# Two-layer memory hybrid in split fp32: how norms are summed and broadcast, where the forget gates are computed, and which instructions open a stage

## The chip, the cores and the metric

The kernel runs on one core of one Trainium2 chip. The metric is the device time of one execution in microseconds, as the median of several runs; the profile is of one more execution.

## The reference

A sequence of 512 tokens, width 1024, in fp32, goes through two layers, each a mixing step and a feed-forward step, all with RMS norms before and after:

```
for layer in range(2):
    a, mem_n = rmsnorm(h, ln_mix_pre[layer]), rmsnorm(mem, ln_mem[layer])
    if layer == 0:      # layer A
        u, v, q_mem = split(a @ w_in_a)                     # 768, 768, 256
        main = gelu(u) * (tril(w_s) @ layernorm(gelu(v)) + b_s)   # 6 groups, chunks of 128
    else:               # layer B
        k, v, f = split(rmsnorm(h, ln_shared) @ w_shared_kv)      # 768, 768, 12
        log_f = log_sigmoid(f + b_forget)                   # 12 heads
        q, q_mem = split(a @ w_in_b)                        # 768, 256
        c = cumsum(log_f)
        main = softmax(q k / 8 + c_t - c_s, causal) @ v     # forgetting attention
    mixed = concat(main, memory_attention(q_mem, mem_n, w_mem_kv))  # 4 heads, 256 memories
    h = h + rmsnorm(mixed @ w_out, ln_mix_post)
    f = rmsnorm(h, ln_ffn_pre)
    f = (silu(f @ w_gate) * (f @ w_up)) @ w_down            # inner width 2816
    h = h + rmsnorm(f, ln_ffn_post)
```

## The kernel before

Every large product is made of three products of split numbers: each fp32 value is held as a high part and a remainder, and `mm3` (lines 193 to 195) adds high x high, low x high and high x low in PSUM. The weights arrive from memory as `raw` blocks (queue of SyncE, SP, four buffers), ScalarE (ACT) casts the high part (`whi`, line 241) and VectorE (DVE) subtracts it (`wlo`, line 242). TensorE is PE below, GpSimd POOL. The program is written in Tile: the order of the code gives priorities, and a scheduler sets the order of instructions on each engine. `tc.issue_after(x)` pins the instructions in its block behind instruction `x`; `tc.high_priority()` lets them go ahead of what is written earlier.

The stages, in order:

- **Layer A.** Tokens and query weights are loaded and split as they come; the query product is made; then blocks of `v` (value_block, pieces of 12 matmuls), taken from a queue named `fill` wherever other work would leave PE waiting. The norm `pre` sums squares over the width (`add`), `finish` turns them with matmuls against a matrix of averages into one number a token (`st`, line 284) and raises it to -1/2 on POOL (`rsqrt`, line 256), `spread` broadcasts it over the partitions by a matmul against the identity (`rb`, line 252) and copies it. A second norm does the same for the memory.
- **Boundaries** (function `boundary`, three of them). `tail(tb)` closes the output product of a token block: DVE adds (line 770), ACT squares with a sum (773), DVE makes the variance `v` (775), POOL the power, ACT scales (792). `turn` transposes the scaled rows on PE (`yt`, line 799), adds them to `h` (804) and prepares the next stage's inputs, with squares folded by `PairNorm` (lines 311 and 313). `group` runs the next projection's first blocks, with `finish` behind it.
- **Feed-forward.** Gate and up products use seven block products instead of eight (class `Seven`): `sums` (lines 944 to 949) makes sums of weight blocks on DVE, `run` the products, `end` the output sums (lines 982 to 985). The hidden width goes in groups; between two groups stands part of the down product `y`. `sevens` runs one pair of blocks, gate and up.
- **Layer B.** Queries, then the forget gates, keys and values, the four memory heads and the twelve heads of the forgetting attention. The gates are a product of their own: `w_f` split into 24 columns (`wfs`), 16 matmuls `f` (line 1185), four transposes `zt` (1190), sums and bias into `z` (1201); then log-sigmoid on ACT and DVE (1204 to 1216: absolute value, exponential, logarithm, corrections), six pieces of `fill`, and the cumulated sum `cs` by matmuls with a triangle (1223), whose parts `cc` go by DMA into the rows 66:68 and 64:66 of the heads' operands `qc` and `kc` (1254, 1255). The heads' softmax uses the exponential on ACT (`mp`, `p`, line 432), `mlg` are the memory heads' logits, `tr` the transposes of the probabilities, `mo` and `o` the products with values. ACT loads a table of functions where the function changes.

## Time and profile before

| | us |
|---|---|
| median of 3 runs | 1131.65 |
| lowest, highest run | 1131.46, 1133.57 |
| profiled execution, span from first to last instruction | 1130.7 |
| mean granted TensorE clock in it | 0.999 |

The profiled execution is given by its span alone; the runs are timed on the device around such a span. How to read the rows: a row of a timeline has the start and the duration in us, engine, line, operation, output and inputs, and in brackets how long the engine sat idle before it and what ended that. A row of groups ends in count, busy time in us, mean ns of one, and idle time ahead. A row of the chain has start, length and what ran. Matmuls overlap: a 128x256 one takes 0.28 us from issue to its modelled end, and the next one starts 0.12 us after it.

### The profile page before, as it was taken

Reading aid. Unit: us, or ns where it says so; the run is one execution under the profiler, and the core shown is the slowest. Engines: PE = TensorE matmul, PEld = TensorE weight load, DVE = VectorE, ACT = ScalarE, POOL = GpSimd, SP = SyncE. Lnnn points to the kernel's source line nnn. Section 1 sums busy time; section 2 is a strip of 40 time slices with the busy share of each in tenths; the row PEclk is TensorE's granted clock in tenths of the full one; section 3 lists DMA queues with packets and bytes.
Section 4 is the critical chain, followed back from the end, with each engine's and each line's share of the span. In section 5 each row is a group of like instructions: output and inputs, shape, how many; then the busy total and the mean of one; then the engine's idle time right before and its main releaser. Section 6 shows DMA issues by size and latency. Waiting matters only on the chain.

```text
span 1130.7 us, 19666 instructions
## 1 busy us (share of the span) xinstructions
PE 1116.5 (99%) x7470; PEld 1015.8 (90%) x7471; DVE 893.1 (79%) x1717; ACT 662.2 (59%) x1385; POOL 24.7 (2%) x42
## 2 busy tenths in 40 slices
PE   9999999999999999999999999999999999999997
PEld 6998889999899898998988898889999899898995
DVE  7878558897698587796858889958998688588775
ACT  8774468664365264476637667768765266254453
POOL 1000000000000000000000000000000000000000
PEclk9999999999999999999999999999999999999999
DMA  7513222334134223343323455521224234133222
GB/s 262 159 38 113 89 79 76 112 111 132 57 112 149 64 87 112 98 152 107 96 93 90 112 128 135 137 75 57 68 102 150 75 104 135 62 112 113 75 75 75
DMA packets 63559, 118.14 MB, mean 104 GB/s; under 512 B 5164, under 2 KB 39992, under 8 KB 63464
## 3 DMA queue, kind: packets, MB, share of 16 engines
q1 hardware_dynamic: 62584, 116.05, 33.1%
q8 instruction: 59, 0.97, 0.3%
q0 software_dynamic: 192, 0.52, 0.2%
q10 hardware_dynamic: 688, 0.31, 0.1%
q14 instruction: 36, 0.29, 0.1%
HBM read 104.71 MB, written 2.10 MB: 94 GB/s over the span
## 4 chain that ended last, share of the span: by engine, by line
PE 88%; DVE 4%; ACT 3%; issue 2%; DMA 2%; POOL 1%; SPq 0%; POOLq 0%; DVEq 0%
PE y L195 9%; PE y L194 9%; PE y L193 9%; PE a L195 5%; PE a L194 5%; PE a L193 5%; PE ps L193 4%; PE ps L195 4%; PE ps L194 4%; PE e L193 3%; PE e L195 3%; PE e L194 3%; PE x L195 3%; PE x L194 3%; PE x L193 3%
## 5 line engine op out<-in xcount | busy, mean ns | idle before, releaser
L241 ACT CAST whi<-raw 128x512 fp32r<-128x512 f32 x460 | 276.7, 620 | 271.4 <-PE y L195 111.3
L242 DVE TENSOR_TENSOR wlo<-raw,whi 128x512 fp32r<-128x512 f32 x460 | 305.6, 685 | 113.2 <-ACT whi L241 109.2
L193 PE MATMUL y<-whi,fhi 128*128 128x512 f32 (+1 forms) x356 | 138.5, 390 | 0.9 <-DVE s L983 0.6
L194 PE MATMUL y<-wlo,fhi 128*128 128x512 f32 (+1 forms) x356 | 138.0, 388 | 0.3 <-DVE wlo L242 0.3
L195 PE MATMUL y<-whi,flo 128*128 128x512 f32 (+1 forms) x356 | 138.1, 388 | 0.1
L193 PE MATMUL x<-xshi,whi 128*128 128x256 f32 x320 | 90.6, 283 | 0.0
L194 PE MATMUL x<-xslo,whi 128*128 128x256 f32 x320 | 90.6, 283 | 0.0
L195 PE MATMUL x<-xshi,wlo 128*128 128x256 f32 x320 | 90.6, 283 | 0.0
L194 PE MATMUL a<-xslo,whi 128*128 128x256 f32 x320 | 90.5, 283 | 0.0
L193 PE MATMUL a<-xshi,whi 128*128 128x256 f32 x320 | 90.5, 283 | 0.0
L195 PE MATMUL a<-xshi,wlo 128*128 128x256 f32 x320 | 90.4, 283 | 0.0
L193 PEld LDWEIGHTS y<-whi,fhi 128*128 128x128 f32 x356 | 66.9, 188 | 15.4 <-DVE s L983 1.3
L195 PEld LDWEIGHTS y<-whi,flo 128*128 128x128 f32 x356 | 66.9, 188 | 14.6 <-DVE flo L242 1.1
L194 PEld LDWEIGHTS y<-wlo,fhi 128*128 128x128 f32 x356 | 66.9, 188 | 14.3 <-DVE wlo L242 1.2
L193 PE MATMUL ps<-xshi,whi 128*128 128x256 f32 (+1 forms) x224 | 67.8, 305 | 0.0
L195 PE MATMUL ps<-xshi,wlo 128*128 128x256 f32 (+1 forms) x224 | 66.8, 300 | 0.0
L194 PE MATMUL ps<-xslo,whi 128*128 128x256 f32 (+1 forms) x224 | 66.2, 298 | 0.0
L193 PEld LDWEIGHTS a<-xshi,whi 128*128 128x128 f32 x320 | 61.4, 192 | 0.3
L194 PEld LDWEIGHTS a<-xslo,whi 128*128 128x128 f32 x320 | 61.4, 192 | 0.3
L193 PEld LDWEIGHTS x<-xshi,whi 128*128 128x128 f32 x320 | 61.4, 192 | 0.0
L194 PEld LDWEIGHTS x<-xslo,whi 128*128 128x128 f32 x320 | 61.4, 192 | 0.0
L195 PEld LDWEIGHTS x<-xshi,wlo 128*128 128x128 f32 x320 | 61.4, 192 | 0.0
(292 smaller groups left out, 3115.6 us busy)
## 6 DMA issues: line engine op xcount, KB each, us to landing
raw<-in_w_gate SPq DMA_DIRECT2D x44, 512.0 KB, 4.2
raw<-in_w_up SPq DMA_DIRECT2D x44, 512.0 KB, 3.5
raw<-in_w_down SPq DMA_DIRECT2D x44, 512.0 KB, 3.7
raw<-in_w_out SPq DMA_DIRECT2D x16, 512.0 KB, 4.7
raw<-in_w_b_q SPq DMA_DIRECT2D x8, 512.0 KB, 3.5
raw<-in_w_a_v SPq DMA_DIRECT2D x6, 512.0 KB, 6.4
raw<-in_w_a_u SPq DMA_DIRECT2D x6, 512.0 KB
raw<-in_w_v SPq DMA_DIRECT2D x6, 512.0 KB, 3.4
```

The source lines that it names most:

```text
L193: PE.matmul(o, w[0], x[0], start=start, stop=False, skip_group_check=more)
L194: PE.matmul(o, w[0], x[1], start=False, stop=False, skip_group_check=more)
L195: return PE.matmul(o, w[1], x[0], start=False, stop=stop, skip_group_check=more)
L241: A.copy(hi, src)
L242: (eng or V).tensor_sub(lo, src, hi)
```

## The change

1. `broadcast` uses the transposing mode of PE instead of a matmul against the identity: one pass instead of two for each 128x128 block in fp32, at 18 blocks.
2. `PairNorm` folds its two halves with one more DVE add (128x256), so that `st` takes one matmul a token block instead of two (two passes instead of four). `finish` of a boundary's first half moves into `group`, behind its seventh step, and `group` gets a lag of 3.
3. Layer A: the squares of `pre` are pinned behind the last token's parts; its statistics are finished and spread once for all 512 tokens instead of in two halves, one value piece apart; the memory norm's `finish` comes three value pieces ahead of its `spread`. Value blocks that end before the statistics are queued (`evacs`).
4. Boundaries: the first two weight blocks are taken behind tail 0's weight parts, and the last tail's sums and scaling get high priority (`urgent`).
5. Feed-forward: the weight sums of a group's first block are pinned behind the last output sum of the group before (`opens`, `ended`); this holds for three groups a layer.
6. Forget gates: the 12 columns of `w_f` are appended to value block 0, whose matmuls become 268 columns wide; `z` is taken from its PSUM rows. The products `f`, the transposes and their copies are gone. The log-sigmoid (`forget`) stands among the memory heads' pieces after the second, the cumulated sum (`cumulate`) after the third, and the six pieces ahead of the heads move among them.

```diff
@@ -238,19 +238,25 @@
                 nc.sync.dma_start(dst, src)
 
     def split(src, hi, lo, eng=None):
-        A.copy(hi, src)
-        (eng or V).tensor_sub(lo, src, hi)
+        last_parts[:] = A.copy(hi, src), (eng or V).tensor_sub(lo, src, hi)
 
     def scaled_parts(src, g, hi, lo):
 
-        A.activation(hi, src, AF.Copy, scale=g)
-        V.scalar_tensor_tensor(out=lo, in0=src, scalar=g, in1=hi, op0=ALU.mult, op1=ALU.subtract)
+        last_parts[:] = (A.activation(hi, src, AF.Copy, scale=g),
+                         V.scalar_tensor_tensor(out=lo, in0=src, scalar=g, in1=hi, op0=ALU.mult, op1=ALU.subtract))
+
+    @contextmanager
+    def behind(some):
+
+        with ExitStack() as s:
+            for ins in some:
+                s.enter_context(tc.issue_after(ins.ins))
+            yield
 
     def broadcast(r4, tbs, o, c0):
 
         for tb in tbs:
-            PE.matmul(o[:, tb * P - c0 : (tb + 1) * P - c0], r4[:, tb : tb + 1].to_broadcast([P, P]),
-                      ident, start=True, stop=True)
+            PE.transpose(o[:, tb * P - c0 : (tb + 1) * P - c0], r4[:, tb : tb + 1].to_broadcast([P, P]), ident)
 
     def rsqrt(dst, src, n):
         G.tensor_tensor(out=dst, in0=src, in1=mhalf[:, :n], op=ALU.pow)
@@ -309,12 +315,14 @@
             c0, c1 = cols
             self.sq[j, cols] = prob("sq", (P, 2, 256))
             A.activation(self.sq[j, cols], h[:, 2 * j : 2 * j + 2, c0:c1], AF.Square)
+            t = self.sq[0, cols]
             if j:
-                V.tensor_add(self.sq[0, cols], self.sq[0, cols], self.sq[j, cols])
+                V.tensor_add(t, t, self.sq[j, cols])
+            if j == KT // 2 - 1:
+                V.tensor_add(t[:, 0, :], t[:, 0, :], t[:, 1, :])
 
         def sums(self, tb, cols):
-            c = slice(tb * P - cols[0], (tb + 1) * P - cols[0])
-            return [self.sq[0, cols][:, x, c] for x in range(2)]
+            return [self.sq[0, cols][:, 0, tb * P - cols[0] : (tb + 1) * P - cols[0]]]
 
 
     h = cp.tile([P, KT, T], F32, name="h")
@@ -596,9 +606,15 @@
                 for k in range(4 * kh, 4 * kh + 4):
                     mm3(o[tk], (a[k][0][:, c], a[k][1][:, c]), w[k], k == 0, k == KT - 1)
                 if kh:
-                    if tk % 2 == 0:
-                        vg[j, tk // 2] = plain("vg", (P, 2, 256))
-                    A.activation(vg[j, tk // 2][:, tk % 2, :], o[tk], AF.Copy, scale=pre.r4[:, tk : tk + 1])
+                    evacs.append(lambda: evacuate(tk))
+                if pre.done:
+                    while evacs:
+                        evacs.pop(0)()
+
+            def evacuate(tk):
+                if tk % 2 == 0:
+                    vg[j, tk // 2] = plain("vg", (P, 2, 256))
+                A.activation(vg[j, tk // 2][:, tk % 2, :], o[tk], AF.Copy, scale=pre.r4[:, tk : tk + 1])
 
             return load, [lambda tk=tk, kh=kh: piece(tk, kh) for tk in range(TB) for kh in range(2)]
 
@@ -611,30 +627,29 @@
                     end = mm3(o, w[k], a[k], k == 0, k == KT - 1)
                     if k == 0:
                         idle(2, zero, end)
-            for f in take(fill, 1):
-                f()
-            for k in range(KT):
-                pre.add(h[:, k, :])
-            for cols in HALVES:
-                pre.finish(cols)
+            def pieces(n):
+                for f in take(fill, n):
+                    f()
+
+            pieces(1)
+            with behind(last_a):
+                for k in range(KT):
+                    pre.add(h[:, k, :])
+            pieces(2)
+            pre.finish(FULL)
+            pre.done = True
             memt = load_mem()
-            for f in take(fill, 1):
-                f()
-            for cols in HALVES:
-                pre.spread(cols, rbc)
+            pieces(1)
+            pre.spread(FULL, rbc)
             qf = [plain("q") for _ in range(2)]
             for f, o in zip(qf, outs):
                 V.scalar_tensor_tensor(out=f, in0=o, scalar=0.125, in1=rbc, op0=ALU.mult, op1=ALU.mult)
             norm = mem_sums(memt)
-            for f in take(fill, 3):
-                f()
+            pieces(1)
             xs = mem_inputs(0, memt)
             wk = mem_key_weights(0)
-            for f in take(fill, 2):
-                f()
             norm.finish((0, NMEM))
-            for f in take(fill, 1):
-                f()
+            pieces(3)
             norm.spread((0, NMEM), rmem)
             V.tensor_copy(r4m, norm.r4[:, :2])
             q = [(act("q"), act("q")) for _ in range(2)]
...
+        def urgent(tb):
+            return tc.high_priority() if tb == TB - 1 and not last else ExitStack()
...
@@ -867,15 +889,19 @@
             c0, c1 = HALVES[half]
             return [tuple(t[:, c0:c1] for t in xs[k]) for k in range(KT)]
 
-        for tb in range(3):
-            tail(tb)
+        tail(0)
+        phase_parts = tuple(last_parts)
+        tail(1)
+        with behind(phase_parts):
+            ws = [block(n) for n in range(2)]
+        tail(2)
         turn(0, range(2))
         tail(3, lambda: turn(0, (2,)))
         turn(0, (3,))
-        ws = [block(n) for n in range(4)]
-        outs = group(ws, inputs(0), h0, ["mm", "lg"] * 2, lag=4,
-                     after={3: lambda: turn(1, range(2)), 5: lambda: turn(1, range(2, 4))})
-        nnorm.finish(h0)
+        ws += [block(n) for n in range(2, 4)]
+        outs = group(ws, inputs(0), h0, ["mm", "lg"] * 2, lag=3,
+                     after={3: lambda: turn(1, range(2)), 5: lambda: turn(1, range(2, 4)),
+                            6: lambda: nnorm.finish(h0)})
         nnorm.spread(h0, dst)
         evac(outs, h0)
         outs = group(ws[:2], inputs(1), h0, ["mm", "lg"])
@@ -982,15 +1008,20 @@
             V.tensor_add(s2[:, left], self.q, s2[:, left])
             V.tensor_add(s2[:, right], self.p, s2[:, right])
             self.rows(1, s2)
-            V.tensor_add(s1, self.x, s1)
+            end = V.tensor_add(s1, self.x, s1)
             self.rows(0, s1)
-
-    def sevens(pair, plain_first):
+            ended[0] = end
+
+    ended = [None]
+
+    def sevens(pair, plain_first, opens=False):
 
         if not plain_first:
             for make in pair:
                 u = make()
-                u.sums()
+                with behind(ended if opens else ()):
+                    u.sums()
+                opens = False
                 for n in (1, 7, 2, 6, 4, 3, 5):
                     u.run(n)
                 u.end()
...
-                                      lambda row, t: up_rows(row, t, fs))), m == 2)
+                                      lambda row, t: up_rows(row, t, fs))), m == 2, m == k0)
...
@@ -1148,86 +1179,83 @@
         def value_block(j):
 
             w, o = [], []
+            width = 256 + (0 if j else HEADS)
 
             def load():
                 for kh in range(2):
-                    w.extend(prepared(i["w_v"][j, kh], (4, 256)))
+                    if j:
+                        w.extend(prepared(i["w_v"][j, kh], (4, 256)))
+                        continue
+                    raw = loaded(i["w_v"][j, kh]).rearrange("p (a b) -> p a b", b=256)
+                    for x in range(0, 4, 2):
+                        pair = [t.rearrange("p (a b) -> p a b", a=2) for t in pair_of_parts(2 * width)]
+                        k = 4 * kh + x
+                        split(raw[:, x : x + 2, :], *(t[:, :, :256] for t in pair))
+                        split(wf[:, k : k + 2, :], *(t[:, :, 256:] for t in pair))
+                        w.extend(tuple(t[:, y, :] for t in pair) for y in range(2))
...
+                    if j == 0:
+                        V.scalar_tensor_tensor(out=z[:, tk, :], in0=o[tk][:, 256:], scalar=r4b[:, tk : tk + 1], in1=bf,
+                                               op0=ALU.mult, op1=ALU.add)
...
-        for k in range(KT):
-            w = wfs[:, k, :, :].rearrange("p a b -> p (a b)")
-            for x in range(2):
-                PE.matmul(o[:n2, :], w, s_act[k][x], start=(k, x) == (0, 0), stop=(k, x) == (KT - 1, 1))
...
-        for f in take(fill, 6):
-            f()
...
@@ -1271,7 +1300,9 @@
 
         ys, outs = out_part(1, mixed)
         more = queue(outs)
-        between = {n: take(fill, c) for n, c in enumerate((3, 3, 4, 4, 4, 4, 4, 4, 3, 3, 3, 3))}
+        between = {n: take(fill, c) for n, c in enumerate((5, 5, 5, 5, 4, 4, 4, 4, 3, 3, 3, 3))}
+        between[1].insert(4, forget)
+        between[2].insert(3, cumulate)
         for n, c in zip(range(12, 17), (2, 3, 3, 4, 4)):
             between[n] = take(more, c)
         assert not fill and not more
```

What the scheduler makes of it is shown at three places. First DVE at the opening of a feed-forward group in layer A (the fourth group). `raw` are weight blocks, `s_17` the sum of two of them, `s_16` the output sums of the block before. Before:

```order
L242 TENSOR_TENSOR wlo_5307<-raw_5304,whi_5306 128x512
L944 TENSOR_TENSOR s_17_5355<-raw_5346,raw_5348 128x512
L946 TENSOR_TENSOR raw_5348<-raw_5348 128x512
L983 TENSOR_TENSOR s_16_5059<-a_5056,s_16_5059 128x256
L985 TENSOR_TENSOR s_16_5058<-x_5055,s_16_5058 128x512
L1038 SCALAR_TENSOR_TENSOR s_16_5059<-s_16_5059,s_15_4922 128x512
L1040 TENSOR_TENSOR s_16_5058<-s_16_5058,s_15_4921 128x512
```

and now:

```order
L241 TENSOR_TENSOR wlo_5303<-raw_5296,whi_5302 128x512
L1009 TENSOR_TENSOR s_16_5051<-a_5048,s_16_5051 128x256
L1011 TENSOR_TENSOR s_16_5050<-x_5047,s_16_5050 128x512
L1069 SCALAR_TENSOR_TENSOR s_16_5051<-s_16_5051,s_15_4914 128x512
L1071 TENSOR_TENSOR s_16_5050<-s_16_5050,s_15_4913 128x512
L970 TENSOR_TENSOR s_17_5347<-raw_5338,raw_5340 128x512
L241 TENSOR_TENSOR flo_4905<-s_16_5051,fhi_4904 128x512
```

The weight sum moved from ahead of the output sums to four instructions behind. Second, ACT at the boundary behind layer A's mixing, with the last tail: `sq` with `ss` is the last square, `y` the scaling by `r`, `hs` and `xshi` the next stage's inputs. Before:

```order
L859 ACTIVATE hs_1972<-h,gains 128x256 x2
L311 ACTIVATE sq_1979<-h 128x512
L241 CAST xshi_1975<-hs_1972 128x512
L773 ACTIVATE sq_1996,ss_1757<-y_1754 128x512
L859 ACTIVATE hs_2009<-h,gains 128x256 x2
L792 ACTIVATE y_1673<-y_1673,r_1759 128x512
L792 ACTIVATE y_1754<-y_1754,r_1759 128x512
```

and now:

```order
L881 ACTIVATE hs_1986<-h,gains 128x256 x2
L317 ACTIVATE sq_1993<-h 128x512
L793 ACTIVATE sq_2010,ss_1751<-y_1748 128x512
L241 CAST xshi_1989<-hs_1986 128x512
L241 CAST whi_2036<-raw_2034 128x512
L814 ACTIVATE y_1667<-y_1667,r_1753 128x512
L814 ACTIVATE y_1748<-y_1748,r_1753 128x512
```

The last square moved ahead of one cast, and a weight cast took the place of the pair `hs` ahead of the scaling. Third, ACT in layer B, from the gates to the memory heads: `az`, `e`, `l` are the gates' steps, `lfh` the high part of the log gate, `mp` the heads' probabilities. Before:

```order
L1204 ACTIVATE az_6945<-z_6937 128x48
L1205 ACT_TABLE_LOAD
L1205 ACTIVATE e_6946<-az_6945 128x48
L1208 ACT_TABLE_LOAD
L1208 ACTIVATE l_1_6948<-w_1_6947 128x48
L241 CAST lfh_6960<-lf_6958 128x48
L241 CAST vals_6872<-vf_7009 128x4x64
L241 CAST vals_6873<-vf_7009 128x4x64
L1227 CAST cc<-cs_7074 12x512
L1229 ACTIVATE cc<-cc 12x512
L432 ACT_TABLE_LOAD
L432 ACTIVATE mp_7128,sm_7097<-mlg_7129,nmx_7096 128x256
```

and now, between the second and the third memory head:

```order
L440 ACTIVATE mp_7135,sm_6912<-mlg_7158,nmx_6911 128x256
L1230 ACTIVATE az_7180<-z_6900 128x48
L241 CAST vals_6863<-vf_7102 128x4x64
L1231 ACTIVATE e_7181<-az_7180 128x48
L241 CAST whi_7353<-q_6112 128x512
L1234 ACT_TABLE_LOAD
L1234 ACTIVATE l_1_7183<-w_1_7182 128x48
L241 CAST pT_7216<-tr_7215 128x512
L440 ACT_TABLE_LOAD
L440 ACTIVATE mp_7224,sm_6914<-mlg_7225,nmx_6913 128x256
L241 CAST pT_7237<-tr_7236 128x512
L440 ACTIVATE mp_7224,sm_6914<-mlg_7245,nmx_6913 128x256
```

The gates' steps moved from ahead of the heads to between their exponentials, with the table of the logarithm loaded there and the other one loaded back.

More of the change, by code (lines that the diff above doesn't have):

```diff
@@ L790, in tail @@
                 return end
[L791 to L792 removed]
+            with urgent(tb):
+                for y in ys[tb]:
+                    A.activation(y, y, AF.Copy, scale=r[:, c])
         return tail, ys
@@ L1219, in layer_b @@
-        cs = ps("mm", s="cs")
-        for tb in range(TB):
-            n = T - tb * P
-            for part in (lfh, lfl):
-                PE.matmul(cs[:HEADS, tb * P :], part[:, tb, :], tri[:, :n],
-                          start=(tb == 0 and part is lfh), stop=(tb == TB - 1 and part is lfl))
-        cc = tp.tile([P, T], F32R, tag="acc", name="cc", bufs=2)
-        ch, cl, nh, nl = (cc[32 * n : 32 * n + HEADS, :] for n in range(4))
-        A.copy(ch, cs[:HEADS, :])
-        V.tensor_sub(cl, cs[:HEADS, :], ch)
@@ new lines, in cumulate @@
+        def cumulate():
+            cs = ps("mm", s="cs")
+            lfh, lfl = sums["parts"]
+            for tb in range(TB):
+                n = T - tb * P
+                for part in (lfh, lfl):
+                    PE.matmul(cs[:HEADS, tb * P :], part[:, tb, :], tri[:, :n],
+                              start=(tb == 0 and part is lfh), stop=(tb == TB - 1 and part is lfl))
+            cc = sums["cc"] = tp.tile([P, T], F32R, tag="acc", name="cc", bufs=2)
+            ch, cl, nh, nl = (cc[32 * n : 32 * n + HEADS, :] for n in range(4))
+            A.copy(ch, cs[:HEADS, :])
+            V.tensor_sub(cl, cs[:HEADS, :], ch)
+            A.activation(nh, ch, AF.Copy, scale=-1.0)
+            V.tensor_sub(nl, ch, cs[:HEADS, :])
```

103 lines of the change are left out of this document (45 added, 58 removed).

## The prediction

> **What bounds the kernel now.** First, from the page of before, the busy shares and the shares of the chain that ended last:
>
> ```profile
> PE 1116.5 (99%) x7470; PEld 1015.8 (90%) x7471; DVE 893.1 (79%) x1717; ACT 662.2 (59%) x1385; POOL 24.7 (2%) x42
> ```
> ```profile
> PE 88%; DVE 4%; ACT 3%; issue 2%; DMA 2%; POOL 1%; SPq 0%; POOLq 0%; DVEq 0%
> ```
>
> TensorE (PE) is busy 99% of the 1130.7 us span and makes 88% of the chain. The kernel is a queue of matmuls: its time falls by what leaves that queue and by what the queue no longer waits for. Second, the waits of PE, longest first (total us, times, longest):
>
> ```profile
> PE yt L799 <- ACT y L792: 1.4, 3, 0.6
> PE idle L88 <- DVE zeros L80: 1.3, 1, 1.3
> PE mlg L465 <- ACT mp L432: 1.0, 1, 1.0
> PE rb L252 <- POOL r L256: 0.9, 2, 0.7
> PE y L193 <- DVE s L983: 0.6, 1, 0.6
> ```
>
> All but the start (`idle`) stand at places that the change touches. Each is understated: a wait is counted from the modelled end of the matmul before it, while the queue lost time from the moment at which the next one would normally have started. Third, therefore, the timelines around these places, by starts.
>
> **The work that leaves PE.** The forget gates, in PE's timeline:
>
> ```profile
> 584.92 0.40 PE L1185 MATMUL f<-shi,wfs 128*24 128x512 f32 x1
> 585.15 0.40 PE L1185 MATMUL f<-slo,wfs 128*24 128x512 f32 x1
> ```
> ```profile
> 588.61 0.28 PE L193 MATMUL v<-whi,shi 128*128 128x256 f32 x1
> 588.73 0.28 PE L194 MATMUL v<-wlo,shi 128*128 128x256 f32 x1
> ```
> ```profile
> 589.65 0.42 PE L1190 MATMUL zt<-ident,zr 24*128 24x24 f32 x4
> 590.00 0.39 PE L195 MATMUL v<-whi,slo 128*128 128x256 f32 x1
> ```
>
> The 16 `f` matmuls hold the queue from 584.92 to 588.61, 3.7 us; the four `zt` transposes from 589.65 to 590.00, 0.35 us. Both go. Instead the 96 matmuls of value block 0 (4 token blocks x 8 k x 3 products) are 268 columns wide. The next start follows 0.23 us after 512 columns (584.92 to 585.15) and 0.12 us after 256 (588.61 to 588.73): 0.11/256 us = 0.43 ns a column, so 96 x 12 columns cost 0.5 us. No row has 268 columns. The ends are no cost at all and the price of 512 columns, 96 x 0.11 = 10.6 us; I take 0.5, because 268 lies next to 256, and keep 10.6 for a rival. Net of this part: 3.7 + 0.35 - 0.5 = 3.5 us.
>
> The norms, in the timeline and, for the counts, in the groups of PE:
>
> ```profile
> 190.84 0.95 PE L284 MATMUL st<-avg,sq 128*128 128x1 f32 x8
> 191.65 0.36 PE L193 MATMUL ps<-xshi,whi 128*128 128x256 f32 x1
> ```
> ```profile
> 197.48 0.60 PE L252 MATMUL rb<-ident,r 128*128 128x128 f32 x4
> 197.84 0.47 PE L193 MATMUL y<-whi,fhi 128*128 128x512 f32 x1
> ```
> ```profile
> 606.65 1.03 PE L448 MATMUL tr<-ident,mp 128*128 128x128 f32 x8
> 607.44 0.48 PE L193 MATMUL k<-shi,whi 128*128 128x512 f32 x1
> ```
> ```profile
> L252 PE MATMUL rb<-ident,r 128*128 128x128 f32 x36 | 5.9, 285 | 0.9 <-POOL r L256 0.9
> L284 PE MATMUL st<-avg,sq 128*128 128x1 f32 x48 | 5.7, 240 | 0.0
> ```
>
> Eight `st` passes hold PE for 0.81 us. There are 48, six sets (two halves at three boundaries), and four of each eight go: 6 x 0.4 = 2.4 us. The DVE add that folds the two halves is 128x256, and one of that shape takes 0.42 us (L983, quoted below), six times. The chain that ended last shows its cover, the last fold of squares of a half and the sums behind it:
>
> ```profile
> 170.95 0.60 DVE sq L313
> ```
> ```profile
> 183.67 0.79 PE st L284 x8
> ```
>
> Twelve microseconds of projection lie between; with that cover gone the adds would cost 6 x 0.42 = 2.5 us.
>
> A broadcast (`rb`) of one block is two passes now; four hold PE for 0.36 us, 0.09 each. As a transpose it is one. The transposes `tr` of the memory heads hold it for 0.79 us by eight, 0.10 each. So 36 x 0.09 = 3.2 us become 18 x 0.10 = 1.8, and 1.4 us go. A transposed broadcast operand stands in no row; the ends are 0 and 1.6 (18 passes gone at 0.09), and I take 1.4 from the nearest row, `tr`.
>
> PE work removed: 3.5 + 2.4 + 1.4 = **7.3 us**. It is work of the queue itself, so it counts whole unless the queue waits anew.
>
> **The waits.** (1) The last tail at a boundary, in the timeline:
>
> ```profile
> 171.11 0.63 ACT L773 ACTIVATE sq<-y 128x512 bf16<-128x512 f32 x1
> ```
> ```profile
> 172.07 0.21 DVE L775 SCALAR_TENSOR_TENSOR v<-ss,rms_eps 128x1 f32<-128x1 f32 x1
> ```
> ```profile
> 172.82 0.28 PE L194 MATMUL ps<-xslo,whi 128*128 128x256 f32 x1
> 173.72 0.88 PE L799 MATMUL yt<-ident,y 128*128 128x128 f32 x6 [0.61 <-ACT y L792]
> ```
>
> PE should have gone on at 172.94 and went on at 173.72: 0.8 us, 0.17 more than the view's 0.61; the three of the group are so 1.4 + 3 x 0.17 = 1.9 us. In the new order of ACT the last square stands one cast (0.5 us) earlier; between it and the scaling lie two casts, about as long as the way over DVE and POOL (171.11 to 172.94 less the square's own time). So up to 0.5 us of each goes, **1.3 us** together (the shortest can't give all), and 0.6 is left. (2) The memory head's table:
>
> ```profile
> 600.40 1.28 ACT L432 ACT_TABLE_LOAD   x1
> ```
> ```profile
> 601.69 0.47 ACT L432 ACTIVATE mp<-mlg,nmx 128x256 f32<-128x256 f32 x1
> ```
>
> ACT loads the exponential's table behind the copies of the cumulated gates, and PE waits 1.0 us for that softmax. Now the heads begin before any gate's logarithm, with the table loaded ahead of the first logits: **1.0 us** goes. (3) The wait of `rb` for POOL, 0.9 us: the memory norm's statistics now lie three value pieces ahead of its broadcast (36 matmuls x 0.12 = 4.3 us), so this goes. By starts it is a little more, so I count **1.1 us**. (4) A group's opening:
>
> ```profile
> 437.28 0.39 PE L195 MATMUL y<-whi,flo 128*128 128x512 f32 x1
> 438.30 0.50 PE L193 MATMUL y<-whi,fhi 128*128 128x512 f32 x1 [0.63 <-DVE s L983]
> ```
> ```profile
> 436.49 0.69 DVE L944 TENSOR_TENSOR s<-raw,raw 128x512 f32<-128x512 f32 x1 [1.07 <-DMA raw<-in_w_gate]
> 437.22 0.69 DVE L946 TENSOR_TENSOR raw<-raw 128x512 f32<-128x512 f32 x1
> 437.83 0.42 DVE L983 TENSOR_TENSOR s<-a,s 128x256 f32<-128x256 f32 x1
> ```
>
> DVE stands 1.07 us for a weight block of the next group, then sums it, and only then finishes the products that PE needs: PE starts 1.02 us after its last start instead of 0.23. With the sums behind, 0.8 us goes here, and a little behind it: **1.0 us**. (5) At layer B's entry the same by way of ACT:
>
> ```profile
> 513.54 0.39 PE L195 MATMUL y<-whi,flo 128*128 128x512 f32 x1
> 514.16 0.49 PE L193 MATMUL y<-whi,fhi 128*128 128x512 f32 x1 [0.23 <-ACT whi L241]
> 514.97 0.50 PE L194 MATMUL y<-wlo,fhi 128*128 128x512 f32 x1 [0.31 <-DVE wlo L242]
> ```
>
> PE loses 0.4 + 0.6 us, counted from its normal 0.23 us between starts. ACT's queue holds casts of layer B's query blocks ahead of the tail's weights that PE waits for; these now stand behind: **0.9 us**. Together 1.3 + 1.0 + 1.1 + 1.0 + 0.9 = 5.3 us.
>
> Against it new waits. Layer A's two halves of statistics become one with a POOL power of four columns, and one value piece (12 x 0.12 = 1.4 us) lies between it and the broadcast; a 128x4 power takes 1.3 us on POOL, so there can be half a microsecond more. The value evacuations wait for that. ACT and DVE run in another order around each moved piece. From 0 to 3 us (the size of all that PE waits for here now); I take **1.0 us**.
>
> **The sum.** 7.3 + 5.3 - 1.0 = 11.6 us, on the span 1130.7 - 11.6 = 1119.1. The median of the runs, 1131.65, lies 0.95 us above the span, so **1120.0 us**.
>
> **Rivals.** *A: the work goes, the waits move.* A scheduler that reorders a whole program may end each wait and make another; then 7.3 us go, less up to 2: 1124.3 to 1126.3. For it: the waits are short, and DVE at 79% has slack but not much. Against: each has one cause in the rows, and the cause is moved.
>
> *B, slower: the pinned sums come too late.* The weight sums of the opening block now stand behind the last product sum, four DVE instructions later (4 x 0.6 = 2.4 us). The raw buffer is given back as much later, and the following load with its 4 to 5 us of landing. Six openings (three a feed-forward layer) at 2.4 us are 14.4 us, more than all that is won: 1120.0 + 14.4 = 1134.4. It decides once PE needs the block's sums less than 2.4 us after they were ready before. Against it:
>
> ```profile
> 458.51 0.28 PE L193 MATMUL a<-xshi,whi 128*128 128x256 f32 x1
> ```
>
> After the wait at 437 PE has the `y` of the old group to do until 458.51, 20 us.
>
> *C: the gates' logarithm between the exponentials.* The chain of the gates now runs between the second memory head's exponentials and the third's, with a load for the logarithm and one back. Each is 1.28 us, and the next ACT instruction starts 0.01 us behind it (600.40 + 1.28 = 601.68, and 601.69), so ACT loses 2.6 us where the softmax passes through it; the order leaves only some short matmuls as cover there, about 1 us as I estimate from their 0.12 us, so up to 1.6 us of it reaches PE: 1121.6. The Trainium skill ("ScalarE: Activation LUTs", "What ACT_TABLE_LOAD costs") counts 1.38 us of drain with each load, 2.66 us a switch. By it the two would cost 5.3 us and, past the same cover, 4.3 us: 1124.3. The row shows the 1.28 us but no idle time behind it; a drain ahead of it no run here separates.
>
> *D: the change doesn't do what it says.* If 268 columns are charged like 512 (10.6 us instead of 0.5), the time is 1130.1; if transposed broadcasts save nothing, 1121.4.
>
> **Chances.** Forecast, 1117 to 1122: 0.56. A 0.25, C 0.09 (inside the range), D 0.05, B 0.05. The range reaches down to **1116**, with no new wait and some unnamed ones mended, and up to **1126**, A with most of its new waits; left out are B, half of D and the edges, some 0.15. A measurement of this kernel tells 0.2%, 2.3 us, from no change. Faster by more: forecast, A, C and half of D, 0.92; same 0.03 (268 columns); slower 0.05 (B).
>
> **What would show it.** PE's page line should lose some 8 us of busy time. `f` and `zt` should be gone, `rb` be 18 and `st<-avg,sq` 24, and the `v` of value block 0 start 0.125 us apart. Waits of PE for `mp`, `r` and `s` should be gone and those for the scaled `y` half as long. I am wrong if PE waits in the memory heads for `pT` or at `cs` for `lfh`, if DVE waits for weight blocks at the openings and PE behind it, or if 268 columns start 0.2 us apart.

## The result, and the profile after

The changed kernel takes 1121.4 us, the median of 4 runs (1120.93 to 1122.15), against 1131.56 for the kernel before: a ratio of 0.9909, 95% interval 0.9895 to 0.9924. The forecast was 1120.0 us, 1116 to 1126. The profiled execution spans 1119.7 us, 11.0 less than before. On its page the busy shares and the shares of the chain:

```profile
PE 1107.3 (99%) x7409; PEld 1002.7 (90%) x7409; DVE 892.0 (80%) x1721; ACT 660.3 (59%) x1388; POOL 28.5 (3%) x41
```
```profile
PE 86%; DVE 7%; ACT 3%; issue 2%; POOL 1%; DMA 1%; SPq 0%; POOLq 0%; DVEq 0%; ACTq 0%
```

PE lost 9.2 us of busy time and stays the bound. One number on this line went up that the prediction never looked at: POOL is busy 28.5 us, 24.7 before, with one instruction fewer. The waits of PE, the longest first:

```profile
PE rb L259 <- POOL r L262: 2.5, 4, 1.7
PE idle L88 <- DVE zeros L80: 1.3, 1, 1.3
PE yt L821 <- ACT y L814: 1.0, 2, 0.5
PE ps L193 <- ACT whi L241: 0.7, 1, 0.7
PE e L193 <- ACT s L1003: 0.4, 1, 0.4
```

The waits for the table (`mp`), for the output sums (`s`) and for layer B's weights are gone. Those for the scaled rows (`yt`) fell from 1.4 to 1.0, not to half as was expected, and the wait of the broadcasts for POOL rose from 0.9 to 2.5, where it should have vanished.

To see where along the program the 11 us lie, the same matmul is looked up in both timelines of PE, and the difference of the starts is taken:

| the place | start before | start after | difference |
|---|---|---|---|
| behind the memory norm's broadcast, layer A (`ps<-mparts,wlo`) | 37.19 | 38.31 | +1.1 |
| ahead of the last tail, first boundary (`ps<-xshi,wlo`) | 172.01 | 174.54 | +2.5 |
| behind the second broadcast, first boundary (`y<-whi,fhi`) | 197.84 | 199.14 | +1.3 |
| layer B's entry, late (`y<-whi,fhi`) | 515.54 | 514.77 | -0.8 |
| behind the second boundary (`ps<-xshi,whi`) | 568.48 | 566.27 | -2.2 |
| layer B's output product (`y<-wlo,mixedhi`) | 745.96 | 738.55 | -7.4 |
| behind the third boundary (`y<-whi,fhi`) | 795.10 | 787.05 | -8.0 |
| the last `idle` matmuls | 1121.87 | 1112.67 | -9.2 |
| the end of the span | 1130.7 | 1119.7 | -11.0 |

The part of the work with the forget gates gives 5.2 us, the three boundaries 1.2, 1.4 and 0.6, the group openings and layer B's entry 2.1, the second feed-forward layer 1.2. Layer A loses 2.5: 1.1 up to the memory norm's broadcast and 1.4 behind it. Of the 1.4, 1.0 has nothing to do with layer A's new order: in the run below that widens the tiles of the weight parts and changes nothing else, the same matmul ahead of the last tail stands at 173.09 instead of 172.01, and the one behind the memory norm's broadcast at 37.25 instead of 37.19. And 1.8 us lie behind the last `idle` matmuls, where the change does nothing.

### The profile page after: what moved, and what is told of

The parts are those of the page before. It is cut to its first block, busy times and chain, and to the rows that moved or that the text cites. A ratio compares the mean times of both kernels' runs of the same rounds, so it can differ in the third digit from the quotient of the medians.

```text
span 1119.7 us, 19536 instructions
## 1 busy us (share of the span) xinstructions
PE 1107.3 (99%) x7409; PEld 1002.7 (90%) x7409; DVE 892.0 (80%) x1721; ACT 660.3 (59%) x1388; POOL 28.5 (3%) x41
## 4 chain that ended last, share of the span: by engine, by line
PE 86%; DVE 7%; ACT 3%; issue 2%; POOL 1%; DMA 1%; SPq 0%; POOLq 0%; DVEq 0%; ACTq 0%
PE y L193 9%; PE y L195 9%; PE y L194 9%; PE a L194 5%; PE a L193 5%; PE a L195 5%; PE ps L195 3%; PE ps L194 3%; PE ps L193 3%; PE e L193 3%; PE e L194 3%; PE x L194 3%; PE x L193 3%; PE x L195 3%; PE e L195 3%; DVE wlo L241 2%
```

## The terms, each as it ran

**The work that left PE** went as forecast. The new columns, the sums of a norm (four passes) and a broadcast (two blocks), each with the matmul that follows:

```profile
583.36 0.28 PE L193 MATMUL v<-whi,shi 128*128 128x268 f32 x1
583.48 0.28 PE L194 MATMUL v<-wlo,shi 128*128 128x268 f32 x1
583.60 0.29 PE L195 MATMUL v<-whi,slo 128*128 128x268 f32 x1
```
```profile
192.85 0.50 PE L290 MATMUL st<-avg,sq 128*128 128x1 f32 x4
193.21 0.37 PE L193 MATMUL ps<-xshi,whi 128*128 128x256 f32 x1
```
```profile
199.01 0.38 PE L259 MATMUL rb<-ident,r 128*128 128x128 f32 x2
199.14 0.48 PE L193 MATMUL y<-whi,fhi 128*128 128x512 f32 x1
```

A 268-column matmul gives way after 0.12 us; over all 96 the mean is 0.1237, so the columns cost 96 x 0.0037 = 0.35 us (forecast 0.5). The `st` set takes 0.36 instead of 0.81 us, six times 0.45 = 2.7 (forecast 2.4). The broadcast of two blocks takes 0.13 us here, 0.36 before; nine such pairs give up to 2.1 (forecast 1.4). With the 4.0 us of `f` and `zt` some 8.5 us went; 7.3 were forecast.

**The table** was loaded where the order said, and cost PE nothing. ACT's timeline between the heads:

```profile
601.39 0.62 ACT L241 CAST whi<-q 128x512 fp32r<-128x512 f32 x1 [0.37 <-PE k L194]
602.03 1.28 ACT L1234 ACT_TABLE_LOAD   x1
603.32 0.24 ACT L1234 ACTIVATE l<-w 128x48 f32<-128x48 f32 x1
603.47 0.57 ACT L241 CAST pT<-tr 128x512 fp32r<-128x512 f32 x1
604.06 1.28 ACT L440 ACT_TABLE_LOAD   x1
605.35 0.47 ACT L440 ACTIVATE mp<-mlg,nmx 128x256 f32<-128x256 f32 x1
```

Each load takes 1.28 us, begins 0.02 us behind the cast ahead of it and ends 0.01 us ahead of the next instruction. So the drain that the Trainium skill ("ScalarE: Activation LUTs", "What ACT_TABLE_LOAD costs") adds to each load, 1.38 us, isn't there on either side. PE waits for none of this: no wait for `mp`'s exponential is left in its list, and the one for the normalised `mp` in the list's tail is 0.3 us in layer A.

**POOL's power** is the term that came out on the wrong side. At the memory norm, the sums on PE with the matmul that follows, the power on POOL, DVE from the sums on, and the broadcast on PE:

```profile
29.02 0.95 PE L290 MATMUL st<-avg,acc 128*128 128x1 f32 x8
29.83 0.37 PE L193 MATMUL v<-whi,ahi 128*128 128x256 f32 x1
```
```profile
34.49 2.89 POOL L262 TENSOR_TENSOR r<-var,mhalf 128x2 f32<-128x2 f32 x1 [7.56 <-DVE var L292]
```
```profile
29.88 2.06 DVE L246 SCALAR_TENSOR_TENSOR mparts<-mem,gains,mparts 128x256 fp32r<-128x256 f32 x5
31.86 2.49 DVE L241 TENSOR_TENSOR wlo<-raw,whi 128x512 fp32r<-128x512 f32 x4
34.27 0.15 DVE L292 TENSOR_SCALAR var<-st 128x2 f32<-128x2 f32 x1
34.34 2.48 DVE L241 TENSOR_TENSOR wlo<-raw,whi 128x512 fp32r<-128x512 f32 x4
```
```profile
37.44 0.43 PE L259 MATMUL rb<-ident,r 128*128 128x128 f32 x2 [1.73 <-POOL r L262]
```

Two things came together. PE was done with the sums (`st`) at 29.83, but DVE made the variance `var` from them only at 34.27, 4.4 us later and behind nine other instructions (3.0 us later in the kernel before); by then the three value pieces that were to cover the way had run, and PE had work to 35.56. And the power took 2.89 us; the same shape took 1.19 before, and 0.69 to 0.70 at its shortest in both traces. It ran beside four subtractions on DVE and was done 0.56 us after the last of them.

Going through all powers in the two traces, the length goes with the DVE instruction that is running when the power starts. If there is none, or one of which an operand comes from PSUM (`h<-yt,...`, `y<-y`), a 128x1 power takes 0.54 to 0.57 us. If it is a subtraction or sum whose two operands both lie in SBUF (`xslo`, `wlo`, `hs`, `sq`), it takes 0.87 to 0.93, and a 128x2 one 0.98 to 2.89. The Trainium skill ("SBUF — State Buffer", "Who interferes with whom") says just that: a DVE instruction with two SBUF inputs contends with a GpSimd instruction that reads SBUF, and the second to issue waits until the first is done. By that alone the power would have been held for one subtraction. So it was at 555.54, where three subtractions follow each other too (1.08 us); at 194.20 it was held for two instructions (1.42 us), and here for four. What decides this, no run shows.

The same happened at the first and the third boundary, where the prediction counted 0.5 us each for the square that moved up:

```profile
174.15 0.21 DVE L795 SCALAR_TENSOR_TENSOR v<-ss,rms_eps 128x1 f32<-128x1 f32 x1
174.28 0.68 DVE L241 TENSOR_TENSOR xslo<-hs,xshi 128x512 fp32r<-128x512 f32 x1
```
```profile
174.44 0.92 POOL L262 TENSOR_TENSOR r<-v,mhalf 128x1 f32<-128x1 f32 x1 [7.52 <-DVE v L795]
```

Before, DVE stood idle beside this power and it took 0.54; now a subtraction starts 0.16 us ahead of it, and of the time won 0.4 us went back. By starts PE lost 0.77 and 0.76 us at these two boundaries before and loses 0.67 and 0.68 now. At the second boundary no such subtraction runs when the power starts; it keeps its 0.54 us, and PE's 0.4 us there are gone.

**The opening of a group** runs as planned: DVE's sums of the output come first, the weight sum (L970) last.

```profile
438.49 0.41 DVE L1009 TENSOR_TENSOR s<-a,s 128x256 f32<-128x256 f32 x1
438.82 0.68 DVE L1011 TENSOR_TENSOR s<-x,s 128x512 f32<-128x512 f32 x1
439.42 0.68 DVE L1069 SCALAR_TENSOR_TENSOR s<-s,s 128x512 f32<-128x512 f32 x1
440.02 0.68 DVE L1071 TENSOR_TENSOR s<-s,s 128x512 f32<-128x512 f32 x1
440.62 0.68 DVE L970 TENSOR_TENSOR s<-raw,raw 128x512 f32<-128x512 f32 x1
```

## The experiments

My theory, formed from the trace: the work counted whole, as forecast; of the waits, those whose cause was an order of DVE or ACT went, and those that hang on POOL's power did not, since DVE's subtractions hold it up. The rivals: the waits simply moved somewhere else; or the pins and the priority themselves cost what is missing.

**Layer A as before.** `layer_a` of the kernel before, all else of the changed one.

```diff
-            with behind(last_a):
-                for k in range(KT):
-                    pre.add(h[:, k, :])
...
-            pre.finish(FULL)
...
+            for cols in HALVES:
+                pre.finish(cols)
...
             norm.finish((0, NMEM))
-            pieces(3)
+            for f in take(fill, 1):
+                f()
```

> The changed kernel with layer A's opening as before (two halves of statistics, memory norm finished late). By the prediction's own sum the mended wait for POOL comes back, 0.9 us, less 0.5 us of dearer statistics: 1121.8 us. By the theory formed from the trace (a power on POOL is held up while DVE runs instructions with two operands in SBUF, so that the memory norm's power took 2.89 us after and 1.19 us before) the new order costs 1 us or more, and this kernel takes 1119.7 to 1120.5 us; the memory norm's wait of PE falls from 1.7 to 0.7 us.

Measured: 1120.34 us (ratio 0.9911, 0.9896 to 0.9925; the changed kernel has 0.9909). The wait fell as the theory said:

```profile
35.01 1.19 POOL L262 TENSOR_TENSOR r<-var,mhalf 128x2 f32<-128x2 f32 x1 [10.24 <-DVE var L292]
```
```profile
PE rb L259 <- POOL r L262: 0.9, 4, 0.4
```

The power is at its old 1.19 us and PE's wait for powers at 0.9 in all, 0.4 of it at the memory norm. The time is on the theory's side of 1121.4, not on the prediction's (1121.8), but the intervals overlap: layer A's new order won nothing. That it lost a microsecond rests on one profile of each: at the same matmul in layer A (`rows<-whi,tri`, 100.22 in the changed kernel) this one stands 1.3 us earlier, 0.4 of which it had already while the first tokens were loaded.

**The forget gates as before.** Layer B of the kernel before, part tiles 512 wide.

```diff
+                PE.matmul(o[:n2, :], w, s_act[k][x], start=(k, x) == (0, 0), stop=(k, x) == (KT - 1, 1))
...
-        between[1].insert(4, forget)
-        between[2].insert(3, cumulate)
```

> The changed kernel with the forget gates as before: own matmuls and transposes ahead of the memory heads, value block 0 at 256 columns, all part tiles 512 wide. By the prediction 3.5 us of PE work and 1.0 us of waiting for the table come back: 1121.4 + 4.5 = 1125.9 us. If the logarithm between the heads' exponentials costs what the rival said, up to 1.6 us, only some 3 us come back: 1124.4 us.

Measured: 1125.47 us (0.9947, 0.9934 to 0.9960), 4.1 us above the changed kernel, against 4.5 forecast and 3 with the rival's stall. The wait that the move had removed is back, whole:

```profile
PE mlg L473 <- ACT mp L440: 1.0, 1, 1.0
```

So the rival of the logarithm between the exponentials falls. The 4.1 us aren't the gates alone, since this kernel also has its part tiles back at 512 columns: behind the second boundary it stands 1.2 us ahead of the changed kernel (565.10 against 566.27), at layer B's output product 3.4 us behind it (741.93 against 738.55). In this stretch 4.6 us came back, against 4.5 forecast.

**No pins on the weight sums.**

```diff
-                                      lambda row, t: up_rows(row, t, fs))), m == 2, m == k0)
+                                      lambda row, t: up_rows(row, t, fs))), m == 2)
```

> The changed kernel without the pins on the weight sums of a group's first block. By the prediction the wait at the fourth group comes back, 0.8 to 1.0 us: 1122.3 us, with PE waiting for DVE's output sums at one opening. If late sums cost (the rival with the pins), it is faster than 1121.4 us, by up to 2.4 us an opening.

Measured: 1122.51 us (0.9921, 0.9908 to 0.9934): 1.1 above, as forecast, but with overlapping intervals, and the profile shows less. DVE's order is the old one, yet the load landed earlier against PE's work than in the kernel before:

```profile
437.26 0.69 DVE L970 TENSOR_TENSOR s<-raw,raw 128x512 f32<-128x512 f32 x1 [0.54 <-DMA raw<-in_w_gate]
437.98 0.69 DVE L972 TENSOR_TENSOR raw<-raw 128x512 f32<-128x512 f32 x1
438.59 0.42 DVE L1009 TENSOR_TENSOR s<-a,s 128x256 f32<-128x256 f32 x1
```
```profile
438.60 0.39 PE L195 MATMUL y<-whi,flo 128*128 128x512 f32 x1
439.07 0.50 PE L193 MATMUL y<-whi,fhi 128*128 128x512 f32 x1
```

PE loses 0.47 - 0.23 = 0.24 us at this start, where the row of before had 0.8. Over the whole opening it loses more: ahead of it (`y<-whi,fhi`, 437.14 in the changed kernel) this kernel stands 0.4 us earlier than the changed one, behind it (`y<-whi,flo`, 450.20) 0.2 us later, 0.6 in all. So the pins help by 0.6 us at this opening in one profile of each, and by 1.1 us in the medians; that the rest of the 0.8 came from the earlier load is likely and not shown. The rival with the late sums falls: without the pins the kernel isn't faster.

**The norms as before.** Broadcasts as matmuls, two sums a block, no fold.

```diff
-            PE.transpose(o[:, tb * P - c0 : (tb + 1) * P - c0], r4[:, tb : tb + 1].to_broadcast([P, P]), ident)
+            PE.matmul(o[:, tb * P - c0 : (tb + 1) * P - c0], r4[:, tb : tb + 1].to_broadcast([P, P]),
+                      ident, start=True, stop=True)
...
```

> The changed kernel with the broadcasts as matmuls against the identity and the norms' sums over both halves of the folded squares. By the prediction 2.4 + 1.4 us of PE work come back: 1125.2 us. If the power on POOL sets when PE goes on at each norm, fewer passes beside it only lengthen the wait, and it is 1123 us or less. If transposed broadcasts save nothing, 1123.8 us.

Measured: 1127.27 us (0.9965, 0.9953 to 0.9977), 5.9 us above. Of the 5.7 us between the two spans some 4.2 lie ahead of the last matmuls, against 3.8 forecast and 4.8 by the rows of the changed kernel; the other 1.5 lie behind the last matmul. So the passes count whole, also where PE waits for the power just ahead of them.

**The tile width in the kernel before.** In every run that holds the 268-column block PE's pace was another: the starts of 512-column products stood 232 ns apart instead of 227 (medians), those of 256-column ones 118.3 instead of 120.0 (means without the waits). The change widens the tiles of weight parts from 512 to 536 columns for all that share the tag, so only that was done to the kernel before.

```diff
-        return (wp.tile([P, 512], F32R, tag="hi", name=name("whi"), bufs=8)[:, :n],
-                wp.tile([P, 512], F32R, tag="lo", name=name("wlo"), bufs=8)[:, :n])
+        return (wp.tile([P, 536], F32R, tag="hi", name=name("whi"), bufs=8)[:, :n],
+                wp.tile([P, 536], F32R, tag="lo", name=name("wlo"), bufs=8)[:, :n])
```

> The kernel before with its weight part tiles allotted 536 columns instead of 512 (2144 bytes apart instead of 2048) and nothing else changed. If the place of these tiles sets PE's pace, the starts of 512-column matmuls stand 232 ns apart (227 before) and of 256-column ones 118 ns (120 before), as in every run that holds the 268-column block; 1928 x 5 - 4828 x 1.7 ns leaves the time within 2 us of 1131.4. If something else of the forget gates' part sets the pace, it stays at 227 and 120.

Measured: 1132.78 us (1.0011, 1.0001 to 1.0022), and the pace went over: 232 and 118.3 ns. One stretch of `y` in the kernel before and here:

```profile
277.96 0.39 PE L195 MATMUL y<-whi,flo 128*128 128x512 f32 x1
278.19 0.39 PE L193 MATMUL y<-whi,fhi 128*128 128x512 f32 x1
278.42 0.39 PE L194 MATMUL y<-wlo,fhi 128*128 128x512 f32 x1
278.64 0.39 PE L195 MATMUL y<-whi,flo 128*128 128x512 f32 x1
```
```profile
278.04 0.40 PE L195 MATMUL y<-whi,flo 128*128 128x512 f32 x1
278.28 0.40 PE L193 MATMUL y<-whi,fhi 128*128 128x512 f32 x1
278.51 0.40 PE L194 MATMUL y<-wlo,fhi 128*128 128x512 f32 x1
278.75 0.40 PE L195 MATMUL y<-whi,flo 128*128 128x512 f32 x1
```

Three products take 0.68 us and 0.71. That the allotted width of these tiles sets the pace is shown, since nothing else was changed; whether by where they lie or by what moves behind them isn't. Over the program it nearly cancels: 1928 x 5 = +9.6 us against 4828 x 1.7 = -8.2, and the median rose by 1.4 us (interval 0.1 to 2.5). Stage by stage it doesn't, as layer A's 1.0 us shows.

**Tiles of 544 columns**, a multiple of 64 bytes apart, in the changed kernel; and the same with the parts of the seven products moved by 32 bytes.

```diff
+    def pair_of_parts(n=512, aside=False, off=0):
...
+        return (wp.tile([P, 544], F32R, tag="hi", name=name("whi"), bufs=8)[:, off : off + n],
...
+            pair = pair_of_parts(off=8)
```

> The changed kernel with its weight part tiles allotted 544 columns instead of 536, so that they lie 2176 bytes apart, a multiple of 64 bytes. If it is the 32-byte offset of every second tile that sets the pace, it comes back to 227 and 120 ns; if the larger tile as such, it stays at 232 and 118. The time is within 1.5 us of 1121.4 either way.

> The same at 544 columns, with the parts of the feed-forward layers' seven products moved 32 bytes into their tiles and all others at its start. If the offset sets the pace, the 256-column matmuls of these products stand 118 ns apart or less and the 512-column ones 227: 2880 x 2 to 3 ns and 1800 x 5 ns under the changed kernel's, together some 10 us less than 1121.4: 1111 to 1113 us. If only the place of the whole set counts, nothing is won.

Measured: 1122.62 us (0.9926, 0.9911 to 0.9941) and 1122.83 us (0.9923, 0.9909 to 0.9938). The pace lies between: about 230 and 119.0 ns in both. So it is neither the 32-byte offset of every second tile alone nor the larger tile as such, and the 10 us that the second was to win aren't there. Which property of the address sets the pace stays open.

**No high priority for the last tail.**

```diff
-            return tc.high_priority() if tb == TB - 1 and not last else ExitStack()
+            return ExitStack()
```

> The changed kernel without the high priority of the last tail's steps. By the prediction 0.5 us of waiting at each of three boundaries comes back: 1122.7 us. If the power on POOL is held up by DVE's subtraction that now runs beside it (0.92 us against 0.54), the priority had won next to nothing, and the time stays within 0.5 us of 1121.4.

Measured: 1124.39 us (0.9941, 0.9927 to 0.9956), slower than either theory said. At the boundary itself the theory of the held power was right: with no subtraction beside it the power takes its short time again,

```profile
174.44 0.54 POOL L262 TENSOR_TENSOR r<-v,mhalf 128x1 f32<-128x1 f32 x1 [7.86 <-DVE v L795]
```

and behind the first boundary's second broadcast this kernel is 0.7 us ahead of the changed one (198.46 against 199.14), 0.35 of which it brought from the first loads. So the priority cost 0.35 us at this boundary; by the same count it cost 0.4 at the third and won 0.4 at the second, the one where the power stays short. The kernel loses its time at one opening:

```profile
PE y L193 <- DVE s L1009: 2.6, 1, 2.6
```

There ACT stood 4.30 us for a block of down weights, where the changed kernel's ACT stood 1.32. Whether that is this order or a late load of this execution is the question of the last run but one.

**The memory norm first.** The statistics right behind the squares, and the key weights' subtractions pinned behind the power.

```diff
...
             norm = mem_sums(memt)
+            power = norm.finish((0, NMEM))
             pieces(1)
             xs = mem_inputs(0, memt)
-            wk = mem_key_weights(0)
-            norm.finish((0, NMEM))
+            with behind((power,)):
+                wk = mem_key_weights(0)
             pieces(3)
```

> The changed kernel with the memory norm's statistics taken right after its squares, and the key weights' subtractions on DVE pinned behind its power on POOL. If the power is held up by subtractions with both operands in SBUF (2.89 us in the changed kernel), it now runs beside DVE's products of q, which read PSUM, in about 0.7 us, and PE's wait of 1.7 us at the memory norm's broadcast goes: 1121.4 - 1.7 = 1119.7 us. If something else makes the power long, it stays above 2 us; if the wait only moves to the next step, the time stays at 1121.4.

Measured: 1120.04 us (0.9894, 0.9879 to 0.9908), the fastest of all. On POOL and beside it on DVE:

```profile
28.45 0.71 POOL L262 TENSOR_TENSOR r<-var,mhalf 128x2 f32<-128x2 f32 x1 [1.77 <-DVE var L292]
```
```profile
28.21 0.16 DVE L292 TENSOR_SCALAR var<-st 128x2 f32<-128x2 f32 x1
28.28 1.28 DVE L646 SCALAR_TENSOR_TENSOR q<-ps,rbc 128x512 f32<-128x512 f32 x2
```
```profile
40.81 0.39 PE L194 MATMUL memv<-wlo,mparts 128*128 128x256 f32 x1 [0.89 <-DVE wlo L241]
```

DVE is as busy beside this power as it was beside the long one, but with products that read PSUM: 0.71 us instead of 2.89. The wait of 1.7 us at the broadcast is gone, and 0.9 of it comes back as a wait for a subtraction that now runs later. That the shorter power took the wait away isn't shown by this run: `var` now comes right behind the sums too, and even a power of 2.89 us from 28.45 would have ended at 31.34, 2.4 us ahead of the broadcast at 33.76. At the same matmul in layer A (`rows<-whi,tri`) this kernel stands 1.2 us ahead of the changed one, 0.3 of it from the first loads. It beats both others by its median; against the changed one the intervals overlap.

The same edit with layer A's opening as before:

> The same edit in the kernel with layer A's opening as before (1120.34 us). There the memory norm's broadcast waits least, so at most 0.9 us is left to win by the theory of the held-up power: 1119.4 to 1120.3 us.

Measured: 1121.5 us (0.9906, 0.9889 to 0.9922). The power is short there too (0.69 us), but the profile has a wait of 1.5 us at an opening of the second feed-forward layer and one of 1.0 us for the first tokens, both far from the edit. Inconclusive on the 0.9 us.

**The memory norm first, and no high priority.**

> The kernel with the memory norm's statistics first (1120.04 us) and without the high priority of the last tail's steps. If that priority wins little at the boundaries themselves and the 2.6 us at the first feed-forward group's opening were the chance of one late load, this takes 1119.5 to 1120.5 us and shows no such wait. If the order without the priority makes the down weights late each time, it takes 1122.5 to 1123.1 us, with PE waiting some 2.5 us for DVE's output sums at that opening.

Measured: 1121.53 us (0.9907, 0.9891 to 0.9924; single runs 1120.85 to 1125.28). The profiled execution, the one of 1125.28 us, has the wait again:

```profile
PE y L193 <- DVE s L1010: 3.4, 2, 2.9
```

The other three runs, 1120.85 to 1122.05, are too short to hold it: the shortest run without it, of the kernel with the norm first, is 1119.38 us, and 2.9 more would be 1122.3. So without the priority the down weights can come too late at that opening, but not each time. What the priority is worth is left open: it costs some 0.35 us over the three boundaries in the profiles, and wins up to 3 us by way of a load behind them.

**More instructions for PE.** The stretch from the last matmul to the end had followed the packets of instructions on queue 8 in the profiles up to here: 59 packets and 5.4 to 5.9 us in the kernel before, in the one with the old norms and in the padded one; 58 and 3.9 to 4.0 in the others.

```diff
     idle(10, zero)
+    o = ps("tr", s="idle")
+    for _ in range(80):
+        PE.matmul(o[:, :1], zero[:, :P], zero[:, :1], start=True, stop=True)
```

> The changed kernel with 80 more matmuls of one column at its start, on zeros, which PE runs while it waits for the first loads or just behind; nothing reads them. In the nine profiles so far the stretch from the last matmul to the end of the program is 5.4 to 5.9 us where queue 8 carries 59 packets of instructions (the kernel before and the two that hold most PE instructions) and 3.9 to 4.0 us where it carries 58. If the count of PE instructions sets this, the packets become 59 and the end 5.4 us or more, with a time of 1123 to 1129 us by what the 80 cost themselves; if it was something in the norms' code, they stay at 58 and 3.9.

Measured: 1121.91 us (0.9911, 0.9892 to 0.9931), 59 packets, and an end of 3.95 us. The packets don't set it. The end is long in the three kernels with the old norms and short in all others; why, no run shows.

## Why the prediction was right, and where it wasn't

- **The PE work** (7.3 us forecast, some 8.5 measured) is the bulk of the gain, and its working held term by term. The two experiments that put it back returned 4.6 us in the gates' stretch, with their table, and 4.2 us ahead of the last matmul for the norms.
- **The table** (1.0) and **layer B's entry** (0.9) held: neither wait is left, and the first came back whole when it was undone.
- **The opening of a group** (1.0): the wait is gone; without the pin 0.6 us came back at this opening in the profile.
- **The wait of `rb` for POOL** (1.1 to be won) is the step that failed: at the memory norm it grew from 0.7 to 1.7 us. The prediction set three pieces of PE's work, 4.3 us, against the way from the statistics to the broadcast and followed neither engine on that way. DVE came to `var` 4.4 us behind the sums, so the cover had run out when the power began; and the power, which the sum gave no length at all, was held to 2.89 us. By the times of the trace it took both: a power of 0.70 us from 34.49 would have ended at 35.19, ahead of the 35.56 to which PE had work, and one of 2.89 us right behind the sums at about 33. The other 0.6 of the 1.6 us by which the list grew is 0.3 at layer A's first norm, which the prediction allowed for among the new waits, and 0.3 at two boundaries.
- **The last tail** (1.3 to be won) was too large: 0.6 by starts, 0.4 in the list of waits. At the first and third boundary the power went from 0.54 to 0.92 us, and PE won only 0.1 us at each; at the second it stayed at 0.54, and the wait went.
- **New waits** (1.0 us taken): single ones of 0.2 to 0.7 us in the list of PE (`ps`, `e`, `tr` and `mo`), 1.6 us together, with an old one of 0.4 gone: about the size taken.
- **The pace** of PE is a term that the prediction doesn't have: the 536-column tiles slow the 512-column products and speed up the 256-column ones. In the kernel before, that cost 1.4 us by the median, and by the profile 1.0 us in layer A alone.
- The **waits** together were to give 4.3 us. The work took some 8.5 of the 9.2 us up to the last `idle` matmuls, so all else gave under 1. That the total still fits (11.6 forecast, 11.0 in the profile) is in part luck: it is owed to more work gone than counted and to 1.8 us behind those matmuls that the prediction knew nothing of. The case of rival A, that the waits move, is what half happened; the larger part of what moved, 1.6 us of the list, stands at POOL's powers.

## What to carry to other kernels

Before counting a wait as mended, follow every step of the way that is to be covered on its own engine, in that engine's order, and look at what runs beside it: here 4.3 us of PE's work were spent before DVE came to a step of 0.15 us, and the power behind it took 2.9 us beside DVE's subtractions instead of 0.7. Where a small POOL step lies on the path, put DVE work that reads PSUM beside it, as in the fastest kernel here, and keep subtractions of two SBUF operands behind it. And add up a profile by the starts of the same instruction at a few places of both traces, and of the traces of the experiments: the sum was right here while two of its terms were not, and only so did the part of the tile width show.

## What the runs showed of the hardware that was not expected

- A POOL power of 128x2 took 0.69 to 2.89 us by what DVE ran beside it. It was held for one, two or four DVE instructions in a row, with the same kind of instruction beside it; why, no run shows.
- The allotted width of the weight part tiles (2048, 2144 or 2176 bytes) sets PE's pace for all products that use them: 227, 232 and 230 ns for 512 columns, 120.0, 118.3 and 119.0 ns for 256. At 2048 bytes nine of ten 256-column starts stand exactly 120 ns behind the last one; at 2144 bytes they scatter, with a standard deviation of 2.8 ns.
- The end of the program behind the last matmul took 3.9 or 5.4 to 5.9 us: the longer end goes with the old code of the norms, and the cause is open.
